# First tiles of two experts drawn from token tiles 0 to 5 and multiplied between the last token tile's routing steps

## The chip, the core and the metric

The kernel runs on one core of one Trainium2 chip. The metric is the device time of one execution in microseconds (us): the median of three runs before the change is 941.35, from 939.15 to 944.55. The engines of the core are TensorE (PE in the profile), VectorE (DVE), ScalarE (ACT), GpSimd (POOL) and SyncE (SP). Each runs its own queue of instructions in order; they wait for one another through semaphores. DMAs are issued from the queues of SP, ACT and POOL.

## What is computed

One decoder layer on 1024 tokens of 1024 features. Three mixers (gated linear attention, a convolution, differential attention) read one projection; their outputs are projected back and added to `x`. Then each token is routed to two of 16 experts: the best group of four by one set of logits, then the two best experts in it.

```python
x = x + mix @ w_out
t = rms_norm(x, ffn_norm_g)
# top-1 group of glog, then top-2 experts inside it, weights top_p
for e in range(16):
    hid = silu(t @ w_gate[e]) * (t @ w_up[e])
    y = y + gates[:, e:e + 1] * (hid @ w_down[e])
x = x + y
```

## The kernel before

**Token tiles.** Everything behind the mixers works on eight tiles of 128 tokens. `out_proj` projects one tile; tiles 0 to 2 are fillers in the attention, tiles 3 to 7 run in a loop at the end of `hybrid_kernel`. While tile i is projected, a table `at` calls the routing of the tiles before at given positions among its matmuls: `out_tr` transposes the normed tokens, `out_logits` multiplies them with the router (`plg`), `route_pick` takes the logits `L`, the experts as one-hot rows `O`, and their sum `M`. `route_rank` counts with a matmul (`pr`) how many earlier tokens chose the same expert; `route_slot` turns the rank into one-hot rows `oh` and writes, with matmuls into `pi` and `pst` (`route_static`), which token sits in which slot. For the last tile all this comes behind its projection, and then `route_tab` and `route_map` build the tables of the tiles.

**Expert tiles.** The experts work on 23 tiles of 128 slots, in an order written as a string: P is an expert with a pair of tiles, S an expert with one. The first tile of each of the first `NSTAT` experts is static (its expert is known when the program is built); the others get their expert at run time. One tile is: a gather of 128 tokens by POOL (`moe_gather`, tile `xg`), transposes (`moe_xt`, `pt` to `xT`), 24 matmuls of 128x512 for gate and up (`moe_gu`, `pgu`), `moe_ht`, 12 matmuls for down (`moe_down`, `py`), the weighting into `y`, and a scatter by POOL that adds `y` to the output. The scatters add to the same array, so each waits until the one before has landed.

**Weights.** An expert has three matrices of 1 MB. Each is loaded as `mraw` and split into a high and a low part in fp32r (`mw`): ACT casts a half of 1024 columns (L129), DVE subtracts it (L130), and POOL does one such subtraction of a down matrix. Static experts are loaded through SP, the others through POOL. Ten `mraw` buffers (two pools of 6 and 4) let the loads run three experts ahead of the tiles; there are four pairs of `mw` buffers.

**What sets the order.** TensorE's instructions stand in the order in which the code is written. For the other engines a scheduler orders them by priority when the program is built; `high_priority(offset=-LATER)` puts work behind what is urgent. Once built, the order on each engine is fixed: a load behind a scatter on POOL is issued after that scatter.

Of the kernel before, what the change touches and what calls it, by code (L numbers as in the profile page):

```python
# [18 lines left out]
S = 1024  # L19
D = 1024  # L20
NT = 8
# [3 lines left out]
NSTAT, NPAIR, NSING = 4, 4, 11  # L25
NALW = 2 * NPAIR + NSING
NDYN = NALW + 8
# [9 lines left out]
EARLY = (True, False)  # L37
SP_LOADS = True
# [5 lines left out]
ORDER = 'PSSPSSPSSPSSSSS'  # L44
# [6 lines left out]
RAW_B = 4  # L51
# [6 lines left out]
EX0 = 'Pvvv'  # L58
# [877 lines left out]
def route_consts(K):  # L936
# [24 lines left out]
    v.memset(K.sacc, 0.0)  # L961
    K.selS = c.tile([128, NSTAT], FT, name="selS")
# [9 lines left out]
    v.tensor_scalar(K.e128, pf[:, 1:2], 16.0, None, op0=OP.mult)  # L972
# [20 lines left out]
def route_pick(K, i):  # L993
# [23 lines left out]
    v.tensor_tensor(T.O, K.iota[:, :16].unsqueeze(1).to_broadcast([128, 2, 16]),  # L1017
# [22 lines left out]

def route_rank(K, i):
# [3 lines left out]
    pr = K.psum.tile([128, 512], FT, name="pr", tag="acc", bufs=2)  # L1045
# [42 lines left out]
def route_static(K, i):  # L1088
    T, v = K.ot[i], K.nc.vector
    ps = K.psum.tile([128, 512], FT, name="pst", tag="acc", bufs=2)  # L1090
# [38 lines left out]
def route_map(K):  # L1129
# [6 lines left out]
    sx = c.tile([128, 128], BF, name="seenx", bufs=1)  # L1136
# [41 lines left out]
    K.slots = tables(K, K.selS, NSTAT, "s", K.sg) + K.slots  # L1178
# [7 lines left out]
def raw_tile(K):  # L1186
    rp = K.ring[K.nraw % len(K.ring)]
    K.nraw += 1
    return rp.tile([128, 2048], FT, name="mraw")


def mw_pair(K):
    return [K.mw.tile([128, 4, 2, 256], FR, name=f"mw{x}") for x in range(2)]
# [50 lines left out]
def moe_gather(K, j):  # L1244
    nc = K.nc
    xg = K.xpage.tile([128, D], FT, name="xg", tag="pg")
    K.last_gather = nc.gpsimd.indirect_dma_start(out=xg, out_offset=None, in_=K.td,
# [17 lines left out]
def moe_gu(K, W, xT, mid):  # L1265
    nc, mp = K.nc, K.mp
    ps = K.psum.tile([128, 512], FT, name="pgu", tag="acc", bufs=2)
# [6 lines left out]
    nc.scalar.activation(sg, ps[:, :256], AF.Silu)  # L1274
# [34 lines left out]
def moe_run(K, tiles, ex, main):  # L1309
# [7 lines left out]
    def gather(a):  # L1317
        if a < n:
            xg[a] = moe_gather(K, tiles[a][1])
# [15 lines left out]
    for a in range(3):  # L1335
        gather(a)
    if main:
        late = route_map(K)
        next(late)
        xT[0] = moe_xt(K, xg[0], 2)  # L1340
    with ExitStack() as st:
        for ins in [K.last_gather] + ([K.last_tab] if main else []):
            st.enter_context(K.tc.issue_after(ins))
        for l in range(3):
            loads(l)
        splits(0)
        loads(3)
        splits(1)
        if not main:
            loads(4)  # L1350
    if not main:
        xT[0] = moe_xt(K, xg[0], 2)
    for a in range(n + 1):
        if a < n:
            def mid(m):
                if main and a == 0 and m == MAP_AT:
                    run(late)
                    loads(4)
                if m == HT_AT and a > 0:
# [11 lines left out]
        if a > 0 and (a != n - 1 or DOWN_AT is None):  # L1371
            down(a - 1)
        if a + 2 in begins:
            loads(begins[a + 2] + 3)
# [35 lines left out]
def hybrid_kernel(ctx, tc, inp, out):  # L1410
# [106 lines left out]
    K.ring = [A] * RAW_A  # L1517
    K.nraw = K.nmw = 0
    g = nc.gpsimd
    ex = [Expert(K, e) for e in range(4)]  # L1520
    loads = [(x, a) for x in ex for a in range(3)]
    for x, a in loads[:RAW_A]:
        x.load(a)
    L = NT - 1
    done = 0
    for i in range(NFILL, NT):
        if i + 1 < NT:
            out_prep(K, i + 1, K.page)
        if i == L - 1:
            sx.close()  # L1530
            B = pool(K, so, "mrawB", RAW_B, side="right")
            K.ring += [B] * RAW_B
            for x, a in loads[RAW_A:RAW_A + RAW_B]:
                x.load(a)
# [3 lines left out]
        if done < i - 1:  # L1538
            at[30] = [lambda k=done: route_rank(K, k)]
            at[44] = [lambda k=done: route_slot(K, k)]  # L1540
            done += 1
        if i == L:
            at[34] = [lambda: out_tr(K, L, K.page2, ((0, 4),))]
            at[42] = [lambda: out_logits(K, L, range(0, 4))]
            at[40] = [lambda: route_rank(K, L - 1)]
            at[58] = [lambda: out_tr(K, L, K.page2, ((4, 6),))]
            at[62] = [lambda: route_slot(K, L - 1)]
            at[66] = [lambda: out_logits(K, L, range(4, 6))]
        run(out_proj(K, i, K.page, K.page, True, at))
    out_tr(K, L, K.page2, ((6, 8),))  # L1550
    out_logits(K, L, range(6, KT))
    route_pick(K, L)
    out_last(K)
    route_rank(K, L)
    route_slot(K, L)
    route_tab(K)
    K.slots = [(K.sg[:, a:a + 1],) for a in range(NSTAT)]
    sl.close()
    with ExitStack() as s1:
        K.mw = pool(K, s1, "mwp", 4)  # L1560
        K.mp = pool(K, s1, "mp")
        K.xpage, K.ypage, K.ny = K.page, K.page2, 0

        with tc.issue_after(K.last_exp):
            nc.scalar.preload_act_table_set("silu_and_others")
        def ex0(hf):
            with tc.high_priority(offset=-LATER):
                ex[0].split_gu([{'P': (g, True), 'p': g, 'v': None}[e] for e in EX0], (hf,))

        def gated(hf):  # L1570
            with tc.issue_after(K.last_exp), tc.issue_after(K.last_pool), tc.issue_after(K.last_route):
                ex[0].split_gu([{'P': (g, True), 'p': g, 'v': None}[e] for e in EX0], (hf,))

        for hf in range(2):
            (ex0 if EARLY[hf] else gated)(hf)
        if SP_LOADS:
            for x, a in loads[RAW_A + RAW_B:]:
                x.load(a)
# [30 lines left out]
```

## Time and profile before

| what | value |
|---|---|
| median of three runs | 941.35 us (939.15 to 944.55) |
| profiled execution, its own time | 940.18 us |
| its span in the profile | 938.6 us |
| mean granted clock of TensorE, share of full | 0.931 |
| busy: PE, DVE, ACT, POOL | 818.2, 649.2, 493.7, 165.0 us |
| moved by the DMA engines | 119.29 MB |

The span is the stretch between the first and the last instruction that the profiler recorded; the execution's own time is 1.6 us longer. The busy times are sums over the whole span; what matters for a change is which engine waits in its stretch. The last projected tile ends near 660 us; the expert stage runs from there to the end.

### The profile page before, as it was taken

The page shows a single profiled execution, that of the slowest core. Times are in us where ns is not written, and L with a number is a line of the kernel's source. Part 1 is how long each engine was busy: PE and PEld are TensorE (multiplying, and loading weights), DVE is VectorE, ACT ScalarE, POOL GpSimd, SP SyncE. Part 2 cuts the span into 40 slices and gives each one's busy share as a digit, 9 for nine tenths or more (in the row PEclk, how much of TensorE's full clock was granted, in tenths as well). Part 3 has the DMA queues.
Part 4 walks back from the last instruction along what each step waited for, and adds up shares of the span by engine and source line. Part 5 has one row for each costly group of instructions (what it writes and reads, how often), then busy time and mean ns, then how long its engine had stood idle before and what let it go on. Part 6 is the DMA issues. An engine that isn't in the chain of part 4 may idle for free. (4 is left out here: it accounts for less than half of the span.)

```text
span 938.6 us, 14319 instructions
## 1 busy us (share of the span) xinstructions
PE 818.2 (87%) x5256; PEld 717.1 (76%) x5256; DVE 649.2 (69%) x1441; ACT 493.7 (53%) x1094; POOL 165.0 (18%) x165
## 2 busy tenths in 40 slices
PE   5999999789768998899878899999399999999870
PEld 4999989688658987788767688888278888888750
DVE  6841556988997666768857666666868677687850
ACT  6743516124246565667757554232558667677730
POOL 5100000000000000000000000000537666664221
PEclk9999989669879999999988999999689999999995
DMA  8210101102002002001202218434479999998942
GB/s 261 76 44 2 46 1 28 37 1 63 6 0 69 1 1 68 1 1 41 68 22 59 81 68 348 168 151 187 170 275 344 335 358 305 363 328 273 318 69 45
DMA packets 46007, 119.29 MB, mean 127 GB/s; under 512 B 6670, under 2 KB 26220, under 8 KB 38636
## 3 DMA queue, kind: packets, MB, share of 16 engines
q0 software_dynamic: 13104, 71.31, 23.0%
q1 hardware_dynamic: 28876, 41.15, 13.2%
q10 hardware_dynamic: 3952, 5.86, 1.7%
q8 instruction: 43, 0.70, 0.3%
q14 instruction: 32, 0.26, 0.1%
HBM read 97.33 MB, written 20.97 MB: 126 GB/s over the span
## 5 line engine op out<-in xcount | busy, mean ns | idle before, releaser
L1272 PE MATMUL pgu<-mw,xT 128*128 128x512 f32 x552 | 140.9, 404 | 0.8 <-ACT xT L129 0.8
L130 DVE TENSOR_TENSOR mw<-mraw,mw 128x1024 fp32r<-128x1024 f32 x99 | 120.9, 1256 | 11.3 <-ACT mw L129 10.4
L1272 PEld LDWEIGHTS pgu<-mw,xT 128*128 128x128 f32 x552 | 102.8, 190 | 24.9 <-issue 1.2
L129 ACT ACTIVATE mw<-mraw 128x1024 fp32r<-128x1024 f32 x113 | 112.9, 1052 | 14.4 <-PE pgu L1272 14.4
L251 PE MATMUL psA<-wh,hnh 128*128 128x384 f32 (+1 forms) x320 | 110.2, 344 | 1.0 <-ACT wh L129 1.0
L251 PE MATMUL psA<-wh,hnl 128*128 128x384 f32 (+1 forms) x320 | 110.6, 346 | 0.2 <-DVE xra L110 0.2
L251 PE MATMUL psA<-wl,hnh 128*128 128x384 f32 (+1 forms) x320 | 109.7, 343 | 0.9 <-DVE wl L130 0.9
L881 PE MATMUL psO<-woh,mx 128*128 128x512 f32 (+1 forms) x272 | 86.8, 396 | 3.5 <-DVE mx L130 2.5
L586 DVE SCALAR_TENSOR_TENSOR mix<-mix,par 128x994 f32<-128x994 f32 (+29 forms) x60 | 75.7, 1262 | 2.1 <-ACT mix L583 1.3
L942 POOL IOTA iota<- 128x128 f32 x1 | 0.2, 238 | 434.9 <-DVE mix L614 434.9
L1300 PE MATMUL py<-mw,hT 128*128 128x512 f32 x276 | 67.3, 392 | 4.5 <-DVE y L1304 2.9
L1300 PEld LDWEIGHTS py<-mw,hT 128*128 128x128 f32 x276 | 51.7, 188 | 16.7 <-ACT hT L129 3.9
L251 PEld LDWEIGHTS psA<-wh,hnh 128*128 128x128 f32 x320 | 63.2, 198 | 1.6 <-ACT wh L129 1.3
L251 PEld LDWEIGHTS psA<-wl,hnh 128*128 128x128 f32 x320 | 63.2, 197 | 1.3 <-DVE wl L130 1.2
L251 PEld LDWEIGHTS psA<-wh,hnl 128*128 128x128 f32 x320 | 63.1, 197 | 0.6 <-DVE hnl L130 0.4
L718 DVE TENSOR_REDUCE nm<-sc 128x1 f32<-128x128 f32 (+7 forms) x64 | 46.8, 751 | 21.7 <-PE sc L714 17.8
L720 ACT ACTIVATE e<-sc,nm 128x128 f32<-128x128 f32 (+7 forms) x64 | 47.3, 740 | 25.6 <-DVE nm L718 21.8
L881 PEld LDWEIGHTS psO<-woh,mx 128*128 128x128 f32 x272 | 49.8, 192 | 12.9 <-DVE mx L130 2.9
L260 PE MATMUL psA<-hnh,wl 128*128 128x256 f32 x192 | 57.1, 297 | 0.0
L260 PE MATMUL psA<-hnl,wh 128*128 128x256 f32 x192 | 57.0, 297 | 0.0
L260 PE MATMUL psA<-hnh,wh 128*128 128x256 f32 x192 | 56.1, 292 | 0.2 <-DVE mix L556 0.2
L881 PE MATMUL psO<-wol,mx 128*128 128x512 f32 (+1 forms) x136 | 53.5, 394 | 0.0
(388 smaller groups left out, 1841.8 us busy)
## 6 DMA issues: line engine op xcount, KB each, us to landing
mraw<-in_expert_w_gate_dram POOLq DMA_DIRECT2D x15, 1024.0 KB, 9.1
mraw<-in_expert_w_up_dram POOLq DMA_DIRECT2D x15, 1024.0 KB, 10.2
mraw<-in_expert_w_down_dram POOLq DMA_DIRECT2D x15, 1024.0 KB, 15.2
wraw<-in_w_in_dram SPq DMA_DIRECT2D x64, 128.0 KB
mix<-in_x_dram SPq DMA_DIRECT2D x8, 512.0 KB
wraw<-in_w_out_dram SPq DMA_DIRECT2D x16, 256.0 KB
h<-in_x_dram SPq DMA_DIRECT2D x8, 512.0 KB
out_dram<-h SPq DMA_DIRECT2D x8, 512.0 KB
```

Source lines behind the costliest of these rows:

```text
L129: K.nc.scalar.activation(hi, src, AF.Copy)
L130: (eng or K.nc.vector).tensor_tensor(lo, src, hi.bitcast(FT), op=OP.subtract)
L251: nc.tensor.matmul(ps[:, :n], a[:, k, cs], b[:, k % 2, :n], start=(k == 0 and t == 0), stop=(k == KT - 1 and t == 2))
L260: nc.tensor.matmul(ps, a[:, k % 2, c0:c0 + 128], b[:, k, :], start=(k == 0 and t == 0), stop=(k == KT - 1 and t == 2))
L586: nc.vector.scalar_tensor_tensor(y[:, sh:], z[:, :S - sh], w(t), y[:, sh:], op0=OP.mult, op1=OP.add)
L718: nc.vector.tensor_reduce(nm, scs[m][:, :n], axis=AX.X, op=OP.max, negate=True)
L720: nc.scalar.activation(e[:, :n], scs[m][:, :n], AF.Exp, bias=nm, accum_out=sums[:, u, m:m + 1])
L881: nc.tensor.matmul(ps, a[:, k, :], b[:, k % 4, c0 % 512:c0 % 512 + c1 - c0], start=(k == 0 and t == 0), stop=(k == KT - 1 and t == 2))
L942: g.iota(t, allow_small_or_imprecise_dtypes=True, **kw)
L1272: nc.tensor.matmul(ps, a[:, k, :], b[:, k % 4].rearrange("p a f -> p (a f)"), start=(n == 0), stop=(n == 23))
L1300: nc.tensor.matmul(py[:, c * 512:(c + 1) * 512], a[:, k, :], b[:, k, c * 512:(c + 1) * 512], start=(k == 0 and t == 0), stop=(k == 1 and t ...
```

## The change

The experts are renumbered by a rotation of ten (`ROT`), so that experts 10 to 15 come first; six are static instead of four, and nine single tiles are dynamic instead of eleven. The sum stays 23 tiles. The first tiles of the first two experts are drawn from token tiles 0 to 5 alone (`ECUT`): `route_static` adds up the slots of these in `eacc` with two further fp32 matmuls for each of the six tiles; `route_cut` raises the two experts' counts to a full tile of 128 behind tile 5; `route_early` makes the slots, and two gathers follow while tile 6 is projected. The ranks of tiles 5 and 6 move to an earlier place. `moe` then starts with the gate and up matmuls of these two tiles, and the routing of the last token tile is called between them (`mid0`, `mid1`). There is one pool of six `mraw` buffers, so that loads run two experts ahead; `mw` has six pairs. The splits of experts 0 and 1 and the loads of experts 2 and 3 stand in `hybrid_kernel`; the shares of POOL in expert 0's gate and up splits are gone.

```diff
-NSTAT, NPAIR, NSING = 4, 4, 11
+NSTAT, NPAIR, NSING = 6, 4, 9
+NEARLY, ECUT, ROT = 2, 6, 10
-ORDER = 'PSSPSSPSSPSSSSS'
+ORDER = 'PSSPSSPSSPSSS'
-RAW_B = 4
...
+def route_cut(K):
+    nc, v = K.nc, K.nc.vector
+    pe = K.psum.tile([128, 512], FT, name="pcut", tag="tr")
+    nc.tensor.matmul(pe[:, :16], K.ones, K.seen[:, ECUT, :], start=True, stop=True)
+    d = K.rt.tile([128, NEARLY], FT, name="cutd", bufs=1)
+    v.tensor_scalar(d, pe[:, :NEARLY], -1.0, 128.0, op0=OP.mult, op1=OP.add)
+    v.scalar_tensor_tensor(K.seen[0:1, ECUT, :NEARLY], d[0:1], 0.0, K.seen[0:1, ECUT, :NEARLY], op0=OP.max, op1=OP.add)
...
 def route_static(K, i):
+    early = i < ECUT
     for s in range(2):
-        K.nc.tensor.matmul(ps[:, :NSTAT], T.oh[0][:, s, :], T.os[:, s, :], start=(s == 0), stop=(s == 1))
+        K.nc.tensor.matmul(ps[:, :NSTAT], T.oh[0][:, s, :], T.os[:, s, :], start=(s == 0), stop=(s == 1 and not early))
+    if early:
+        for s in range(2):
+            K.nc.tensor.matmul(ps[:, NSTAT:NSTAT + NEARLY], T.oh[1][:, s, :], T.os[:, s, :NEARLY].bitcast(FT),
+                               start=False, stop=(s == 1))
...
     if main:
+        L = NT - 1
+        xg.update(enumerate(K.xge))
+        xT[0] = K.xt0
+
+        def mid0(m):
+            if m == 4:
+                out_tr(K, L, K.page2, ((6, 8),))
+                out_logits(K, L, range(6, KT))
+                route_pick(K, L)
+                out_last(K)
+            if m == 12:
+                xT[1] = moe_xt(K, xg[1])
+
+        def mid1(m):
+            if m == 2:
+                route_rank(K, L)
+            if m == 12:
+                hid[0] = moe_ht(K, hid[0])
+            if m == 18:
+                route_slot(K, L)
+                route_tab(K)
+                K.slots = K.eslots + [(K.sg[:, a:a + 1],) for a in range(NEARLY, NSTAT)]
+                for a in range(NEARLY, 5):
+                    gather(a)
+
+        hid[0] = moe_gu(K, ex[0].W, xT[0], mid0, wait=lambda: K.last_exp)
+        splits(2)
+        static(4)
+        hid[1] = moe_gu(K, ex[1].W, xT[1], mid1, True)
         late = route_map(K)
         next(late)
+        down(0)
+        splits(3)
+        static(5)
+        hid[1] = moe_ht(K, hid[1])
+        down(1)
+        xT[2] = moe_xt(K, xg[2], 2)
...
         if a + 2 in begins:
-            loads(begins[a + 2] + 3)
+            loads(begins[a + 2] + 2)
...
         if i == L - 1:
             sx.close()
-            B = pool(K, so, "mrawB", RAW_B, side="right")
-            K.ring += [B] * RAW_B
-            for x, a in loads[RAW_A:RAW_A + RAW_B]:
-                x.load(a)
+            K.mwe = pool(K, so, "mwe", 4, side="right")
+            with tc.high_priority(offset=-LATER):
+                ex[0].split_gu()
+                for a in range(2):
+                    ex[2].load(a)
...
-        if done < i - 1:
+        if done < i - 1 or i == L - 1:
             at[30] = [lambda k=done: route_rank(K, k)]
             at[44] = [lambda k=done: route_slot(K, k)]
...
-        K.mw = pool(K, s1, "mwp", 4)
+        K.mw = pool(K, s1, "mwp", 8)
...
+        with tc.high_priority(offset=-LATER):
+            ex[0].split_d((None, None))
+            ex[2].load(2)
+            ex[1].split_gu()
+            for a in range(2):
+                ex[3].load(a)
+            ex[1].split_d((None, None))
+            ex[3].load(2)
         moe(K, ex)
```

The built programs show two places where instructions moved. The first is DVE's queue behind the last token tile's projection; `h` adds the projection's second half, `L` are its logits, `mw<-mraw,mw` is one subtraction of a split. Before:

```order
L889 TENSOR_TENSOR h<-psO_7453,h 128x256
L130 TENSOR_TENSOR mw_7595<-mraw,mw_7594 128x4x256
L897 TENSOR_TENSOR hsum<-hsum,hs 128x1
L107 TENSOR_SCALAR hrv<-hsum 128x1
L109 SCALAR_TENSOR_TENSOR hra<-hry 128x1
L110 TENSOR_TENSOR hra<-hra,hrv 128x1
L112 SCALAR_TENSOR_TENSOR hr<-hra,hry 128x1
L933 SCALAR_TENSOR_TENSOR L<-plg,hr,rb 128x24
```

After the change, from `hrv` on (two more subtractions and `h` stand just ahead):

```order
L104 TENSOR_SCALAR hrv<-hsum 128x1
L127 TENSOR_TENSOR mw_7587<-mraw,mw_7586 128x4x256 x2
L127 TENSOR_TENSOR mw_7593<-mraw,mw_7592 128x4x256 x2
L127 TENSOR_TENSOR mw_7697<-mraw,mw_7696 128x4x256 x2
L106 SCALAR_TENSOR_TENSOR hra<-hry 128x1
L127 TENSOR_TENSOR mw_7603<-mraw,mw_7602 128x1024 x2
L107 TENSOR_TENSOR hra<-hra,hrv 128x1
L127 TENSOR_TENSOR xT<-pt,xT 128x1024
L127 TENSOR_TENSOR mw_7703<-mraw,mw_7702 128x4x256
L109 SCALAR_TENSOR_TENSOR hr<-hra,hry 128x1
L127 TENSOR_TENSOR mw_7703<-mraw,mw_7702 128x4x256
L930 SCALAR_TENSOR_TENSOR L<-plg,hr,rb 128x24
```

One subtraction stood between `h` and `L`; now there are twelve, and a half of `xT`.

The second place is POOL's queue in the expert stage, one cycle of four tiles; `out_dram<-y` is a scatter, `xg` a gather, `mraw` a load. Before, from the loads behind scatter S5 to scatter S7:

```order
L1212 ISA
L1212 DMA mraw<-in_expert_w_gate_dram 128x2048
L1212 ISA
L1212 DMA mraw<-in_expert_w_up_dram 128x2048
L1212 ISA
L1212 DMA mraw<-in_expert_w_down_dram 128x2048
L130 TENSOR_TENSOR mw_8361<-mraw,mw_8360 128x1024
L1305 DMA out_dram<-y,os 1152x1024
L1247 DMA xg<-td,og 128x1024 x3
L1305 DMA out_dram<-y,os 1152x1024
```

After the change, from the gather ahead of scatter S4 to the loads behind S5:

```order
L1283 DMA xg<-td,og 128x1024
L1349 DMA out_dram<-y,ss 1152x1024
L127 TENSOR_TENSOR mw_8363<-mraw,mw_8362 128x1024
L1349 DMA out_dram<-y,ss 1152x1024
L1246 TENSOR_LOAD erow
L1246 ISA x2
L1248 ISA
L1248 DMA mraw<-in_expert_w_gate_dram 128x2048
L1248 ISA
L1248 DMA mraw<-in_expert_w_up_dram 128x2048
L1248 ISA
L1248 DMA mraw<-in_expert_w_down_dram 128x2048
```

Before, three gathers stood between the two scatters that have no loads between them; now nothing but a subtraction stands there, and the cycle's gathers stand with loads: in the next group, behind S6, three loads and three gathers.

## Rows read from the trace of the kernel before

The times are those of the profiled execution. Lines as L1305 are lines of the kernel before.

**Rows 1.** The chain that ended last: start us, us, what.

```profile
915.49 1.55 DMA out_dram<-y,os
```

**Rows 2.** All instructions on out_dram: from a scatter's issue to its landing.

```profile
DMA to landing us min/median/max: 6.3/9.0/11.9
```

**Rows 3.** Timeline of POOL: the scatters into out_dram.

```profile
738.03 2.53 POOL L1305 DMA_INDIRECT out_dram<-y,ss  x1 [1.99 <-DMA out_dram<-y,ss]
...
746.72 1.62 POOL L1305 DMA_INDIRECT out_dram<-y,os  x1 [0.30 <-DVE xT L130]
...
759.45 1.66 POOL L1305 DMA_INDIRECT out_dram<-y,os  x1 [3.08 <-DVE mw L130]
...
769.26 1.67 POOL L1305 DMA_INDIRECT out_dram<-y,os  x1 [3.33 <-DMA out_dram<-y,os]
...
779.12 2.01 POOL L1305 DMA_INDIRECT out_dram<-y,os  x1 [3.93 <-DVE sg L1275]
...
787.74 1.63 POOL L1305 DMA_INDIRECT out_dram<-y,os  x1 [0.30 <-DVE mw L130]
...
799.18 2.10 POOL L1305 DMA_INDIRECT out_dram<-y,os  x1 [4.84 <-DVE mw L130]
...
870.39 1.65 POOL L1305 DMA_INDIRECT out_dram<-y,os  x1 [3.45 <-DVE hT L130]
...
899.37 3.65 POOL L1305 DMA_INDIRECT out_dram<-y,os  x1 [5.12 <-DVE y L1304]
...
922.18 1.55 POOL L1305 DMA_INDIRECT out_dram<-y,os  x1 [5.14 <-issue]
```

**Rows 4.** Timeline of PE in the expert stage: two neighbouring tiles, and a wait.

```profile
768.70 2.98 PE L1272 MATMUL pgu<-mw,xT 128*128 128x512 f32 x12
...
778.19 2.98 PE L1272 MATMUL pgu<-mw,xT 128*128 128x512 f32 x12
...
883.02 3.00 PE L1300 MATMUL py<-mw,hT 128*128 128x512 f32 x12 [2.86 <-DVE y L1304]
```

**Rows 5.** Windows: sum, then busy (instructions) PE, PEld, DVE, ACT, POOL, clock, DMA, GB/s.

```profile
670.00:680.00 10.00, 2.60 (x15) 2.39 (x15) 9.56 (x16) 4.85 (x6) 7.66 (x5) 0.50 0.74 275
...
700.00:720.00 20.00, 20.00 (x98) 16.67 (x97) 17.64 (x20) 17.12 (x23) 12.88 (x11) 1.00 1.01 370
```

**Rows 6.** Timeline of PE: start us, us, line, operation, out<-in, [idle before].

```profile
646.36 1.86 PE L930 MATMUL plg<-wr,hT 128*128 128x24 f32 x16
...
659.82 0.28 PE L881 MATMUL psO<-woh,mx 128*128 128x256 f32 x1
...
682.53 3.75 PE L1272 MATMUL pgu<-mw,xT 128*128 128x512 f32 x8 [0.78 <-ACT xT L129]
...
688.61 1.04 PE L1258 MATMUL pt<-ident,xg 128*128 128x128 f32 x8
689.41 5.86 PE L1272 MATMUL pgu<-mw,xT 128*128 128x512 f32 x24
...
699.50 2.90 PE L1300 MATMUL py<-mw,hT 128*128 128x512 f32 x12
702.24 2.98 PE L1272 MATMUL pgu<-mw,xT 128*128 128x512 f32 x12
```

**Rows 7.** All instructions on mraw: ns min/median/max of the two halves of a split.

```profile
L130 DVE TENSOR_TENSOR mw<-mraw,mw x99: 1210/1217/4057, 660.5 to 900.4; 128x1024 fp32r<-128x1024 f32 x99
```

**Rows 8.** Timeline of DVE around the last token tile.

```profile
660.13 0.42 DVE L889 TENSOR_TENSOR h<-psO,h 128x256 f32<-128x256 f32 x1 [2.34 <-PE psO L881]
...
665.08 0.24 DVE L933 SCALAR_TENSOR_TENSOR L<-plg,hr,rb 128x24 f32<-128x24 f32 x1
...
666.95 0.17 DVE L1020 TENSOR_TENSOR M<-O 128x16 bf16<-128x16 f32 x1
```

**Rows 9.** Timelines of DVE and POOL: two subtractions side by side.

```profile
676.39 4.06 DVE L130 TENSOR_TENSOR mw<-mraw,mw 128x1024 fp32r<-128x1024 f32 x1
677.01 2.35 POOL L130 TENSOR_TENSOR mw<-mraw,mw 128x1024 fp32r<-128x1024 f32 x1
```

More of the change, by code (lines that the diff above doesn't have):

```diff
@@ L1044, in route_rank @@
     T = K.ot[i]
[L1045 removed]
+    pr = K.psum.tile([128, 512], FT, name="pr", **route_tag(i))
     nc.tensor.matmul(pr[:, :16], K.tri, T.M, start=True, stop=(i == 0))
@@ L1186, in raw_tile @@
 def raw_tile(K):
-    rp = K.ring[K.nraw % len(K.ring)]
-    K.nraw += 1
-    return rp.tile([128, 2048], FT, name="mraw")
+    return K.mraw.tile([128, 2048], FT, name="mraw")
 def mw_pair(K):
-    return [K.mw.tile([128, 4, 2, 256], FR, name=f"mw{x}") for x in range(2)]
+    p = K.mwe if K.nmw % 6 < 2 else K.mw
+    K.nmw += 1
+    return [p.tile([128, 4, 2, 256], FR, name=f"mw{x}", tag="mw") for x in range(2)]
 class Expert:
@@ L1262, in moe_xt, with moe_gu @@
     return xT
-def moe_gu(K, W, xT, mid):
+def moe_gu(K, W, xT, mid, wide=False, wait=None):
     nc, mp = K.nc, K.mp
-    ps = K.psum.tile([128, 512], FT, name="pgu", tag="acc", bufs=2)
+    if wide:
+        ps = K.psum.tile([128, 1024], FT, name="pguw", tag="sc")[:, :512]
+    else:
+        ps = K.psum.tile([128, 512], FT, name="pgu", tag="acc", bufs=2)
     order = [(k, t) for hf in range(2) for t in range(2) for k in range(hf * 4, hf * 4 + 4)] + [(k, 2) for k in range(KT)]
@@ L1273, in moe_gu @@
     sg = mp.tile([128, 256], FT, name="sg", bufs=2)
-    nc.scalar.activation(sg, ps[:, :256], AF.Silu)
+    if wait is not None:
+        with K.tc.issue_after(wait()):
+            nc.scalar.preload_act_table_set("silu_and_others")
+            nc.scalar.activation(sg, ps[:, :256], AF.Silu)
+    else:
+        nc.scalar.activation(sg, ps[:, :256], AF.Silu)
     nc.vector.tensor_tensor(sg, sg, ps[:, 256:], op=OP.mult)
@@ L1317, in gather @@
     def gather(a):
-        if a < n:
+        if a < n and a not in xg:
             xg[a] = moe_gather(K, tiles[a][1])
@@ L1333, in down, with static @@
         moe_down(K, ex[tiles[a][0]].W, hid[a], tiles[a][1], main and a >= n - END_PAGE)
-    for a in range(3):
-        gather(a)
+    def static(l):
+        with K.tc.high_priority(offset=-LATER):
+            for a in range(len(ex[l].raws), 3):
+                ex[l].load(a)
     if main:
+        L = NT - 1
[24 more added lines that the diff above has]
+        hid[1] = moe_gu(K, ex[1].W, xT[1], mid1, True)
@@ L1338, in moe_run @@
         late = route_map(K)
         next(late)
-        xT[0] = moe_xt(K, xg[0], 2)
[L1341 to L1353, printed above, removed]
+        down(0)
+        splits(3)
@@ L1354, in moe_run @@
+        static(5)
+        hid[1] = moe_ht(K, hid[1])
+        down(1)
+        xT[2] = moe_xt(K, xg[2], 2)
+    else:
+        for a in range(3):
+            gather(a)
+        loads(0)
+        loads(1)
+        splits(0)
+        loads(2)
+        splits(1)
+        loads(3)
+        xT[0] = moe_xt(K, xg[0], 2)
+    for a in range(2 if main else 0, n + 1):
         if a < n:
             def mid(m):
-                if main and a == 0 and m == MAP_AT:
+                if main and a == 2 and m == MAP_AT:
@@ L1357, in mid @@
                     run(late)
-                    loads(4)
-                if m == HT_AT and a > 0:
+                if m == HT_AT and a - 1 in hid and not (main and a == 2):
                     hid[a - 1] = moe_ht(K, hid[a - 1])
@@ L1516, in hybrid_kernel, with early, early_xt @@
         route_pick(K, i)
-    K.ring = [A] * RAW_A
-    K.nraw = K.nmw = 0
+    K.mraw = A
+    K.nmw = 0
     g = nc.gpsimd
-    ex = [Expert(K, e) for e in range(4)]
-    loads = [(x, a) for x in ex for a in range(3)]
-    for x, a in loads[:RAW_A]:
-        x.load(a)
+    ex = [Expert(K, (e + ROT) % NE) for e in range(NSTAT)]
+    for x in ex[:RAW_A // 3]:
+        for a in range(3):
+            x.load(a)
     L = NT - 1
     done = 0
+    K.xpage, K.ypage, K.ny = K.page, K.page2, 0
+    def early():
+        K.eslots = K.slots = route_early(K)
+        K.xge = [moe_gather(K, a, ECUT * 128) for a in range(NEARLY)]
+    def early_xt():
+        K.xt0 = moe_xt(K, K.xge[0])
     for i in range(NFILL, NT):
```

74 lines of the change are left out of this document (37 added, 37 removed).

## The prediction, made before the changed kernel ran

> **What bounds the kernel now.** I went from the end backwards. The chain of waits ends in the scatters of the expert stage [rows 1]: POOL adds the tokens of one expert tile to the output, and each scatter is issued only when the one before has landed, 6.3 to 11.9 us after its issue [rows 2]. I number the 23 scatters S0 to S22; the rows show S3 to S9, S16, S19 and S22. Between S4 and S16, 12 scatters take 870.39 - 746.72 = 123.67 us, 41.2 us for four [rows 3]. TensorE needs 778.19 - 768.70 = 9.49 us for a tile, 38.0 for four [rows 4]. So the scatters fall behind TensorE by 3.2 us in every four tiles, until TensorE waits for them at 883 (2.86 us behind DVE's `y`, whose page the scatters had not yet left) [rows 4]. The last scatter is issued at 922.18, whatever TensorE does after its last tile. The windows show the other place where time is lost: from 670 to 680 TensorE works 2.60 of 10 us, at half clock; from 700 on it has no gap, while the DMA engines are full (share 1.01, 370 GB/s) [rows 5]. The reader is to see two resources there: a gap of TensorE before the expert stage, which the change aims at, and a queue of transfers behind it, which sets the end.
>
> **Part 1, up to the last output matmul.** It ends at 659.82 + 0.28 = 660.1 [rows 6]. Added ahead of it are: (a) two fp32 matmuls of two columns in each of tiles 0 to 5, 12 in all. They are not in the trace. Sixteen records of `plg`, fp32 with 24 columns, take 1.70 us up to the next start, and one instruction is two records [rows 6], so 0.21 each, 2.5 together; from below 0 (they hide between waits), from above 2.5; I take 2.5 since the matmuls around them leave no gap. (b) The eight transposes of the first expert tile, 689.41 - 688.61 = 0.8 [rows 6], which leave the gap. (c) The rank of tile 5 moves into tile 6, whose position 30 TensorE reaches while DVE has four halves of expert 0 ahead of tile 5's logits, 4 x 1.217 = 4.9 us [rows 7]. How much of this TensorE waits is between 0 and 4.9; ahead of that position stand 30 matmuls, at 5.86 / 24 = 0.24 each 7.3 us, that cover most of it, so I take 1.5. Sum: 660.1 + 4.8 = 664.9. The additions on DVE and the two early gathers lie beside matmuls; without that cover they would cost some 3 us.
>
> **Part 2, the gap.** Before, `L` of the last token tile starts 5.0 us after 660.1, `M` at 666.95 [rows 8], and the third expert tile starts at 702.24 [rows 6], 42.1 after 660.1. In the change the DVE queue holds 12 subtractions of splits between the last `h` and that `L` (ten in the rows shown of the order, two ahead of them), where there was one, and the lower half of `xT`. Twelve more at 1.217 are 14.6 [rows 7]; I take off 3 for the waits on ACT that DVE has between `h` and `L` today and that the splits fill, so `L` comes at 664.9 + 5.0 + 11.5 = 681.4 and `M` 1.9 later, 683.3. TensorE has the first tile's 24 matmuls for this time (5.6 at full clock, 11.3 at the 0.47 of eight in 3.75 [rows 6]); then it stands until `M`, as before. Then come the rest of the second tile (22 matmuls, 5.2 to 10.3, taken as 7), twice 2.90 for `py` [rows 6], and the transposes, copies and waits between: at least three groups of transposes at 0.8, 2.4, at most two waits of 4.06 more [rows 9], 10.5; I take 8.4, near the upper bound, since DVE is busy 9.56 of 10 us there already before [rows 5]. Sum 704.5, between 698 and 710. So the gap is filled with two tiles, but its end is not earlier: +2.3 us. TensorE then has one `py` of 2.90 less ahead than before at this point. **The entry to the expert loop is about even.**
>
> **A rule against the row, on the gap.** In the trace a DVE subtraction that stood beside one of POOL took 4.06 us instead of 1.22 [rows 7, 9]. The Trainium skill, "SBUF — State Buffer", section "SBUF: two separate sides", says that DVE, with two inputs in SBUF, and GpSimd share a pair of ports as an exclusive lock, so that whichever starts first holds off the other for its whole length. The change keeps one POOL subtraction ahead of the gathers of tiles 2 to 4; by that rule this could delay them by up to 2.8 us, and the sum below would be 954 instead of 951. I leave it out, since the rule gives no order of the two.
>
> **Part 3, the expert stage, which sets the end.** I read what stands between two scatters on POOL, and what it made of the next interval (all loads, gathers and scatters that POOL issues share one queue, so a scatter lands behind the loads ahead of it). After an interval with three loads: 9.81 and 9.86 (S5 to S6, S6 to S7). After three loads and one gather: 12.73 and 11.44 (S4 to S5, S8 to S9), mean 12.1. After three gathers alone: 8.62 (S7 to S8). After nothing: (922.18 - 899.37) / 3 = 7.6 [rows 3]. The four make the old cycle: 12.7 + 9.8 + 9.9 + 8.6 = 41.0. It agrees with the bytes: a load is 1.05 MB, at 370 GB/s 2.8 us [rows 5], three and a scatter of 0.52 MB 9.9.
>
> The order of the change on POOL shows other groups: loads run two experts ahead instead of three, out of six raw pages instead of ten. From S3 on a cycle is now three loads and a gather, **nothing**, three loads, then **three loads and three gathers**. The gathers that used the interval without loads now stand in one with loads. Two gathers more cost between 2 x 0.4 (three gathers alone cost 8.6 - 7.6) and 2 x 2.3 (12.1 - 9.8); by bytes 2 x 1.4 = 2.8, which I take. Cycle: 12.1 + 7.6 + 9.8 + 14.9 = 44.4, from below TensorE's 38.0, from above 46.2. Three cycles from S4 to S16: 133.2 against 123.67, **+9.5**.
>
> The end: behind S16 there are now loads of the last expert after S17 instead of after S16. 9.8 + 7.6 + 9.8 + 3 x 7.6 = 50.0 against 922.18 - 870.39 = 51.8: **-1.8**. The start: S3 now has loads, three gathers and a POOL subtraction ahead of it; S4 between -2 and +7 us, I take **+3.3** from one interval of 12.1 where 8.7 was (S3 to S4, 746.72 - 738.03 [rows 3]). The loads of two more experts go over SP and come before; the bytes are the same. The Trainium skill, "DMA: Bandwidth & Descriptors", section "Issuing engines are not separate DMA queues", says that transfers of all engines end up on the same 16 DMA engines; no run here shows the two queues side by side in this stage. By it the move to SP gains nothing, which the share of 1.01 [rows 5] supports.
>
> **Sum.** +3.3 + 9.5 - 1.8 = +11.0. The profiled execution took 940.18 (1.2 below the median of 941.35): 951.2, **951**. TensorE will wait more often for a free `y` page, but its waits are inside this chain.
>
> **Rivals.** (A) The cycle keeps its length, because the loads, issued earlier in some intervals, fill the empty one: 940.2 + 3.3 - 1.8 = 941.7. For it: the bytes are the same, and the DMA engines were already full. Against: POOL issues in order, and nothing stands between those two scatters. Chance 0.20. (B) The gap really closes, and the result is faster: if the 12 subtractions don't hold `L` (because their casts and loads are early and DVE runs through them while TensorE is still in tile 7), 11.5 us go from the gap; the scatters start that much earlier, and with the old cycle the end is 940.2 - 8 = 932. The point that decides is `L` of the last tile: under 8 us behind the last output matmul it is this. Against: `h`, which stands ahead of them on DVE, itself waits for that matmul [rows 8]. Chance 0.10. (C) Six raw pages starve the splits: an expert's loads are issued two tiles, 19.0 us, ahead of use, and the longest group in the queue is 14.9 by part 3; a wait of 2 us in each of the nine single tiles is +18 for TensorE, of which the scatters hide half: 960. Against: the wait at 883 is for `y`, none in the rows is for a load. Chance 0.15. (D) The change doesn't do what it says: a token count beyond the 23 tiles would start the loop for the rest, another expert with some 28 us (12.1 + 9.5 + 7): 968. Nothing in the trace tells it. Chance 0.02. The forecast has 0.53.
>
> **How the numbers follow.** About 0.5% (4.7 us) is what a measurement of this kernel can tell from no change: faster is under 936.6, slower over 946.1. Faster: B, 0.10. Same: A and the low edge of the forecast (a cycle of 42.5 gives 945), 0.22. Slower: 0.68. The range takes A's upper half, the forecast with gathers at both bounds (945 to 957) and C: 940 to 961; outside are B, D and part of A.
>
> **What would show it.** `L` of the last token tile 14 to 18 us behind the last output matmul, not 5; the third expert tile at 701 to 709; a stretch of half clock as long as before; four scatters in 43 to 46 us from S4 to S16, with one interval near 7.6 and one near 15 in each; the loads of the last expert behind S17; the last scatter near 933. If four scatters take 41 us, part 3 is wrong and A holds; if the third tile starts before 696, part 2 is wrong and B holds; if splits wait for loads, C.

## The result and the profile after the change

The changed kernel takes **952.19 us** in the median (949.18 to 954.66) beside 940.25 for the kernel before in the same comparison: a ratio of **1.0138 [1.0103, 1.0174]** (the brackets are a 95% interval), slower by 12 us in the medians and some 13 by the ratio. The prediction was 951, between 940 and 961. The profiled execution took 954.66 (span 952.8), the longest of four and 14.5 more than the profiled one before. Shown are, of both, the places that the prediction named:

| place | before | after | predicted for after |
|---|---|---|---|
| end of the last output matmul | 660.1 | 665.1 | 664.9 |
| `L`, `M` of the last token tile | 665.1, 667.0 | 681.2, 683.1 | 681.4, 683.3 |
| third expert tile starts | 702.2 | 706.4 | 704.5 |
| scatter S4 | 746.7 | 752.4 | 750.0 |
| S4 to S16, twelve scatters | 123.7 | 133.4 | 133.2 |
| S16 to S22 | 51.8 | 51.0 | 50.0 |
| S22 to the end of the execution | 18.0 | 17.8 | not named |

The differences, +5.0 up to the last output matmul, -0.8 from there to the third tile, +1.5 to S4, +9.7, -0.8 and -0.2, make the 14.4 that the profiled executions lie apart.

**The entry.** Timeline of PE in the kernel after the change (start, length, line, operation, idle time before it with its releaser):

```profile
640.67 0.18 PE L1076 MATMUL pr<-M,tri 128*128 128x16 bf16 x1 [1.82 <-DVE M L1025]
...
664.84 0.28 PE L878 MATMUL psO<-woh,mx 128*128 128x256 f32 x1
664.95 1.10 PE L1311 MATMUL pgu<-mw,xT 128*128 128x512 f32 x4
...
683.35 0.19 PE L1076 MATMUL pr<-M,tri 128*128 128x16 bf16 x1 [7.09 <-DVE M L1025]
...
698.55 1.19 PE L1344 MATMUL py<-mw,hT 128*128 128x512 f32 x4 [2.25 <-ACT hT L126]
700.34 3.66 PE L1344 MATMUL py<-mw,hT 128*128 128x512 f32 x8 [0.60 <-DVE hT L127]
...
706.42 2.12 PE L1311 MATMUL pgu<-mw,xT 128*128 128x512 f32 x8 [1.54 <-ACT xT L126]
```

The first expert's matmuls follow the projection at once; later TensorE stands for 7.09 us until `M`. The last row is the start of the third tile. Timeline of DVE over the same time, and the POOL rows that belong to its last one:

```profile
668.56 6.89 DVE L127 TENSOR_TENSOR mw<-mraw,mw 128x1024 fp32r<-128x1024 f32 x6
...
681.24 0.24 DVE L930 SCALAR_TENSOR_TENSOR L<-plg,hr,rb 128x24 f32<-128x24 f32 x1
...
683.12 0.17 DVE L1025 TENSOR_TENSOR M<-O 128x16 bf16<-128x16 f32 x1
...
689.02 3.23 DVE L127 TENSOR_TENSOR mw<-mraw,mw 128x1024 fp32r<-128x1024 f32 x1
...
688.78 2.38 POOL L127 TENSOR_TENSOR mw<-mraw,mw 128x1024 fp32r<-128x1024 f32 x1 [21.49 <-PE pguw L1311]
692.59 0.96 POOL L1283 DMA_INDIRECT xg<-td,sg  x1 [1.43 <-DVE seenx L1173]
```

`L` stands behind the subtractions, as the order said. The 3.23 us of a subtraction beside POOL's answer to the 4.06 of [rows 9]. Two windows of the stretch (columns as in [rows 5]):

```profile
670.00:680.00 10.00, 3.73 (x16) 2.41 (x15) 10.00 (x11) 7.36 (x9) 0.00 (x0) 0.82 0.90 329
680.00:690.00 10.00, 6.65 (x31) 5.58 (x31) 7.83 (x37) 6.07 (x11) 1.22 (x1) 0.67 0.89 341
```

DVE has no gap from 670 to 680, TensorE works 3.73 us of these ten. The granted clock is 0.82 and 0.67 in the mean of these windows, a mixture of its two levels, 1.2 and 2.4 GHz, where [rows 5] had 0.50 in the first. In windows of 2.5 us it is under full from 662.5 to 687.5 before, and from 675 to 687.5 and 700 to 705 after, behind the waits of TensorE. So the stretch at the lower level is shorter than before, while the prediction had it as long.

**The scatter cycle.** Timeline of POOL from S4 to S9, then S16 and S22, where [rows 3] has those of before:

```profile
752.42 1.64 POOL L1349 DMA_INDIRECT out_dram<-y,ss  x1 [1.06 <-DMA out_dram<-y,ss]
...
764.18 2.05 POOL L1349 DMA_INDIRECT out_dram<-y,ss  x1 [5.86 <-DVE mw L127]
765.73 1.12 POOL L1248 DMA_DIRECT2D mraw<-in_expert_w_gate_dram  x1
766.32 1.10 POOL L1248 DMA_DIRECT2D mraw<-in_expert_w_up_dram  x1
766.88 1.06 POOL L1248 DMA_DIRECT2D mraw<-in_expert_w_down_dram  x1
771.45 1.66 POOL L1349 DMA_INDIRECT out_dram<-y,os  x1 [3.51 <-DVE xT L127]
...
777.82 1.01 POOL L1283 DMA_INDIRECT xg<-td,og  x1 [0.30 <-issue]
779.14 0.97 POOL L1283 DMA_INDIRECT xg<-td,og  x1 [0.30 <-issue]
780.42 1.93 POOL L1283 DMA_INDIRECT xg<-td,og  x1 [0.31 <-PE pt L1294]
782.65 1.62 POOL L1349 DMA_INDIRECT out_dram<-y,os  x1 [0.30 <-DVE hT L127]
...
797.06 2.47 POOL L1349 DMA_INDIRECT out_dram<-y,os  x1 [2.15 <-DMA out_dram<-y,os]
...
808.08 1.58 POOL L1349 DMA_INDIRECT out_dram<-y,os  x1 [6.11 <-DVE sg L1319]
...
885.81 2.36 POOL L1349 DMA_INDIRECT out_dram<-y,os  x1 [7.73 <-DVE mw L127]
...
936.84 1.55 POOL L1349 DMA_INDIRECT out_dram<-y,os  x1 [5.16 <-DMA out_dram<-y,os]
```

The three loads stand before S6, three loads (left out) and three gathers before S7, and no transfer stands between S4 and S5. The releasers named are often engines that had long been done: ten of the twelve scatters from S5 to S16 are issued 4.6 us or more behind their `y`, and the wait is for the landing. S7 and S14 are issued 0.5 and 0.3 us behind their `y`, so there the tile may have set the issue. Grouped by what was issued ahead of the interval's first scatter, the twelve intervals from S4 to S16 are:

| ahead | after, three each | predicted |
|---|---|---|
| three loads, one gather | 11.76, 11.02, 12.17 | 12.1 |
| nothing | 7.27, 7.11, 8.69 | 7.6 |
| three loads | 11.20, 11.36, 9.91 | 9.8 |
| three loads, three gathers | 14.41, 13.50, 14.99 | 14.9 |

**What the new order wastes.** The same window of both kernels; the first row is of before, the second of after (columns as in [rows 5]):

```profile
760.00:820.00 60.00, 60.00 (x296) 50.09 (x295) 42.80 (x49) 39.93 (x52) 40.70 (x30) 1.00 1.00 349
```

```profile
760.00:820.00 60.00, 57.68 (x274) 47.98 (x273) 40.48 (x43) 34.32 (x45) 33.53 (x28) 0.97 0.86 288
```

Before, the DMA engines are full all the time. After, they have 0.86 and 288 GB/s. Where nothing stands between two scatters they run dry: from 762 to 766, on both sides of the issue of S5, their share is 0.02, and from 806 to 810, around S9, again. The groups that follow are so much the larger. Part of what an empty interval saves is paid in the next, which has three loads ahead: the two together take 18.5, 18.5 and 18.6 us, where the prediction had 7.6 + 9.8 = 17.4.

### The profile page after: what moved, and what is told of

The parts are those of the page before. It is cut to its first block, busy times and chain, and to the rows that moved or that the text cites. A ratio compares the mean times of both kernels' runs of the same rounds, so it can differ in the third digit from the quotient of the medians.

```text
span 952.8 us, 14375 instructions
## 1 busy us (share of the span) xinstructions
PE 825.8 (87%) x5281; PEld 723.6 (76%) x5281; DVE 661.5 (69%) x1460; ACT 494.5 (52%) x1095; POOL 149.8 (16%) x156
## 3 DMA queue, kind: packets, MB, share of 16 engines
q0 software_dynamic: 12240, 65.02, 21.2%
## 5 line engine op out<-in xcount | busy, mean ns | idle before, releaser
L127 DVE TENSOR_TENSOR mw<-mraw,mw 128x1024 fp32r<-128x1024 f32 x102 | 135.3, 1365 | 31.8 <-ACT mw L126 24.4
L1311 PE MATMUL pgu<-mw,xT 128*128 128x512 f32 x528 | 134.8, 404 | 1.5 <-ACT xT L126 1.5
L1311 PEld LDWEIGHTS pgu<-mw,xT 128*128 128x128 f32 x528 | 99.3, 192 | 23.5 <-ACT xT L126 1.7
L1344 PE MATMUL py<-mw,hT 128*128 128x512 f32 x276 | 72.6, 414 | 10.1 <-ACT hT L126 4.6
L1344 PEld LDWEIGHTS py<-mw,hT 128*128 128x128 f32 x276 | 54.4, 200 | 24.2 <-ACT hT L126 5.4
```

What stands on the lines that cost most here:

```text
L127: (eng or K.nc.vector).tensor_tensor(lo, src, hi.bitcast(FT), op=OP.subtract)
L1311: nc.tensor.matmul(ps, a[:, k, :], b[:, k % 4].rearrange("p a f -> p (a f)"), start=(n == 0), stop=(n == 23))
L1344: nc.tensor.matmul(py[:, c * 512:(c + 1) * 512], a[:, k, :], b[:, k, c * 512:(c + 1) * 512], start=(k == 0 and t == 0), stop=(k == 1 and t ...
```

## The experiments

Ratios are to the kernel before, measured beside it, whose median lay between 936.89 and 942.6 in these comparisons. S0 to S22 are the scatters, a cycle is four of them.

**1. The same kernel with other pages for y.** One number moves the gathers back into the interval without loads.

```diff
-YP = [0, 0, 0, 1]
+YP = [0, 1, 0, 0]
```

> The changed kernel with one table shifted by two places: of four y tiles the second, not the fourth, takes its page from the pool of the gathers. On POOL this puts two gathers into the interval between two scatters that was empty, and takes the three gathers out of the crowded one; loads, raw pages and all matmuls stay. Theory G (grouping on POOL sets the scatter chain): a cycle of four scatters from S4 on falls from 44.5 to 41 or 42 us, three cycles give 5 to 9 us, about 945 us against 952 for the change. Rival S (six raw pages starve the splits): the loads are issued as before, the time stays within 2 us of 952.

Measured: 947.75, ratio 1.0073 [1.0036, 1.0110], 4.4 us less than the change has by the medians and 6 by the ratios. Timeline of POOL, the scatters S4 to S8:

```profile
755.27 1.68 POOL L1349 DMA_INDIRECT out_dram<-y,ss  x1 [4.93 <-DVE y L1348]
...
764.75 1.62 POOL L1349 DMA_INDIRECT out_dram<-y,ss  x1 [0.15 <-issue]
...
772.74 1.64 POOL L1349 DMA_INDIRECT out_dram<-y,os  x1 [0.30 <-issue]
...
785.95 1.66 POOL L1349 DMA_INDIRECT out_dram<-y,os  x1 [6.87 <-DVE xT L127]
...
796.80 2.37 POOL L1349 DMA_INDIRECT out_dram<-y,os  x1 [2.03 <-DVE y L1348]
```

A cycle takes 41.5, 40.7 and 40.3 us: an interval behind two or three gathers alone 8.0 to 8.5, behind three loads 9.5 to 10.9, behind three loads with gathers 12.4 to 13.2. The cycles together gave back 133.4 - 122.5 = 10.9 us; 2.9 of it went again since S4 came later, most of that already ahead of the last output matmul (667.5). Same number of transfers, same bytes, six raw pages in both: what stands with what is the cause of the longer cycle.

**2. The counterpart.** The same line in the kernel before puts its gathers with loads.

> The kernel before with the same table shifted by two places. On POOL one interval of a cycle is now empty and another holds three loads and two gathers, as in the changed kernel; it keeps ten raw pages, loads three experts ahead and its old gap. Theory G: the cycle rises from 41.2 to 44 us, the time by 7 to 10 us to about 949. Rival S: raw pages and lookahead are as they were, the time stays within 2 us of 940.

Measured: 953.05, ratio 1.0121 [1.0071, 1.0170]. Two of three cycles take 44.7 and 44.9 us, the third 40.9. The time came out 4 us above theory G's 949. So one number makes the old kernel as slow as the change, without any of its other edits.

**3 and 4. Scatters that need not wait for one another.** Each expert tile scatters into an array of its own, so that the experts' outputs are left out of the result; otherwise all work stays.

```diff
+    dst = K.dram.tile([S + 128, D], FT, name=f"scr{K.ny}") if K.ny <= 23 else K.out
-    K.last_gather = nc.gpsimd.indirect_dma_start(out=K.out, ...
+    K.last_gather = nc.gpsimd.indirect_dma_start(out=dst, ...
```

> The changed kernel with every scatter adding into an array of its own, so that no scatter waits for the one before; the expert outputs are left out of the result. Theory G: TensorE sets the end. Its last tile starts near 706 + 20 x 9.5 = 896, the last scatter is issued near 912 instead of 937, and the time is about 929. Rival S: waits for loads stay in TensorE's way, 938 or more.

> The kernel before with every scatter adding into an array of its own; the expert outputs are left out of the result. Theory G: the third tile starts at 702 as before and TensorE runs without the wait at 883, the last scatter near 908 instead of 922, about 926 us; so the two kernels without the chain lie some 3 us apart, the difference at the entry, instead of 12. Rival S: the distance of 12 stays.

Measured: the changed kernel 933.82, ratio 0.9917 [0.9887, 0.9947]; the kernel before 927.39, ratio 0.9839 [0.978, 0.9899]. The chain of scatters costs the changed kernel 1.0138 - 0.9917 = 2.2%, 21 us, and the one before 1.6%, 15. By these ratios 6 of the 13 us are the chain's, as in experiment 1, but their intervals leave that uncertain by about as much. Some 6 to 7 remain without the chain, twice theory G's 3: the third tile is 2.1 us later (705.2 and 703.1), and behind it TensorE is 208.8 us, not 204.6, from done. In that stretch its waits add up to 5.8 us, most of them for `sg` and `y`, and to 2.2 in the kernel before; what makes them longer is not tested. What lies outside the cycles the prediction had put at +1.5 (S4 +3.3, tail -1.8).

**5 and 6. The loads on another queue.** The loads of experts chosen at run time are issued by SP; gathers and scatters stay with POOL.

```diff
-    engines=(mybir.EngineType.Pool,),
+    engines=(mybir.EngineType.SP,),
-            self.load(a, self.K.nc.gpsimd)
+            self.load(a, self.K.nc.sync)
```

> The changed kernel with the loads of the experts chosen at run time issued from SP's queue instead of POOL's; scatters and gathers stay on POOL, the bytes are the same. Theory Q (a scatter lands behind the loads that stand ahead of it in the same queue): without them an interval costs what the empty ones cost in the changed kernel, 7.1 to 8.7 us (up to 9 with three gathers), four scatters some 31 to 33, less than TensorE's 38, so the chain no longer sets the end; the time is that of the kernel whose scatters do not wait for one another, about 934, and splits wait for loads as little as there (3 us instead of 16.7). Rival B (bytes: all transfers share the same DMA engines, so it does not matter from which queue they come): four scatters in 43 to 46 as before, 952 within 3.

> The kernel before with the same move of the loads to SP's queue. Theory Q: about 928, as where its scatters do not wait for one another (927.4); four scatters in 38, set by TensorE. Rival B: 941 within 3, four scatters in 40 to 43. In both, the distance to the changed kernel on SP tells what the change costs without the chain: 6 to 7 us by the runs without the chain.

Measured: 951.29, ratio 1.0117 [1.0069, 1.0166], and for the kernel before 945.38, ratio 1.0041 [1.0007, 1.0075]. Nothing is gained that can be told, and before loses a little. The landing of the scatters, first of the changed kernel, then of the same with its loads on SP:

```profile
DMA to landing us min/median/max: 6.0/8.3/11.4
```

```profile
DMA to landing us min/median/max: 6.1/9.0/13.8
```

Two windows of the latter:

```profile
760.00:820.00 60.00, 57.38 (x271) 47.14 (x270) 45.63 (x47) 38.55 (x50) 27.77 (x16) 0.97 1.00 345
...
880.00:930.00 50.00, 41.86 (x189) 33.55 (x187) 27.68 (x32) 22.48 (x32) 11.38 (x7) 0.97 0.56 120
```

From 760 to 820 the DMA engines are now full (1.00, 345 GB/s), no split waits for a load, and still four scatters take 46.7, 45.1 and 41.0 us. What the loads take early, the scatters wait for. The six last intervals, with hardly a load left, take 44.0 instead of 51.0, but S4 comes 5.1 us later, and the median is the same. In the kernel before the move makes the cycles longer, 43.5, 46.8 and 41.7 us instead of 41.0, 39.5 and 43.2, and S4 14.6 us later; its last six intervals take 42.8 instead of 51.8. So theory Q falls, and rival B holds for the changed kernel, while the kernel before is 1.4 us over B's range. The Trainium skill, "DMA: Bandwidth & Descriptors", section "Issuing engines are not separate DMA queues", says that transfers of all engines share the same 16 DMA engines, and these runs agree. So my words that a scatter lands behind the loads of its own queue were too narrow: loads from another queue hold it up as well. Within POOL's queue the order does count: three loads issued 1.6 to 2.7 us behind S5 left that interval at 7.27.

**7. Every y in its own pool.** `YP = [0, 0, 0, 0]` spreads the gathers evenly.

> The changed kernel with every y in its own pool of pages (none in the gathers' pool), which spreads the gathers of a cycle: three loads and one gather, one gather alone, three loads, three loads and two gathers. It measures what a gather beside loads costs. If 2.3 us each (from three loads 9.8 and with one gather 12.1), a cycle is 12.1 + 8.0 + 9.8 + 14.4 = 44.3, no change, 952 within 2. By the intervals of the changed kernel and of the one with its pages shifted (11.9, 7.9, 10.3, 13.2) it is 43.3, 948 to 949. If a gather costs only its bytes, 1.4 each, 11.2 + 8.0 + 9.8 + 12.6 = 41.6, about 944.

The cycles take 42.1, 42.5 and 41.5 us, nearest to the price by bytes (41.6). Their single intervals don't bear it out: three loads alone took 12.40 and 12.14, three loads with two gathers 11.72 and 11.74. So the sum fits, and the price of a gather stays open. Behind an empty interval or a lone gather, three loads cost more than the 9.8 that was read from intervals behind a full one; why is not shown. The time does not show the shorter cycles: 952.3, ratio 1.0103 [1.0057, 1.0149]. In its profile the last output matmul ended at 670.4, 5.3 later than in the changed kernel, though the instructions up to there are the same, and already some 5 later at 605. The time is inconclusive.

**8. No subtraction of POOL ahead of the gathers.**

```diff
-        splits(2)
+        ex[2].splits(True)
```

> The changed kernel with the last half of expert 2's down split on DVE instead of POOL: nothing is left on POOL ahead of the gathers of tiles 2 to 4. Theory L (the two subtractions side by side hold each other off: in the changed kernel DVE's took 3.23 us beside POOL's 2.38, ahead of the tables): the tables and the third gather come 2.0 us earlier, the third tile at 704.4 instead of 706.4, and the scatters behind it with it: 950. Rival N (DVE is full there, and the subtraction that it takes over costs 1.2 before the third tile): third tile at 705 to 707, 952 within 1.

Timelines of DVE, POOL and PE of this kernel:

```profile
688.77 2.35 DVE L127 TENSOR_TENSOR mw<-mraw,mw 128x1024 fp32r<-128x1024 f32 x2
...
691.47 0.96 POOL L1283 DMA_INDIRECT xg<-td,sg  x1 [24.42 <-DVE seenx L1173]
...
704.03 2.14 PE L1311 MATMUL pgu<-mw,xT 128*128 128x512 f32 x8 [1.82 <-ACT xT L126]
```

DVE does two subtractions in 2.35 us, where one beside POOL's had taken 3.23; the gathers start 1.1 us earlier and the third tile 2.4, with the last output matmul at the same place (664.9). That is theory L's number, but only half of it is L's. From `M` to the third tile it is 21.2 us here and 23.3 in the changed kernel. In experiments 1, 3 and 5, which keep POOL's subtraction there, it is 22.3; the difference to the changed kernel is a `py` that ran at the lower clock in the profiled execution (from 700.0 to 702.5 granted 0.56, in experiment 3 1.00; 3.66 us at 700.34 above). The same eight matmuls in experiment 3:

```profile
700.36 2.12 PE L1344 MATMUL py<-mw,hT 128*128 128x512 f32 x8 [0.60 <-DVE hT L127]
```

So the subtraction is worth 1.1 us at the third tile, and the clock 1.0. The execution did not get faster: 954.97, ratio 1.0147 [1.0107, 1.0188]. So the local cost is shown, and that it reaches the end is not.

**9. The logits ahead of the splits.** The splits of experts 0 and 1, with their loads, are called behind `out_last` in `mid0`, and the tables earlier.

```diff
             if m == 4:
...
+                with K.tc.issue_after(K.last_exp), K.tc.high_priority(offset=-LATER):
+                    ex[1].split_gu()
+                    ex[0].split_d((None, None))
...
+            if m == 22:
+                route_rank(K, L)
-            if m == 18:
+            if m == 8:
```

> The changed kernel with the splits of experts 0 and 1 put behind the logits of the last token tile in DVE's order (the loads of expert 2's down and of expert 3 move with them), and the tables called earlier. Theory O (the twelve subtractions ahead of L set the end of the gap by their order): L near 671 instead of 681.2, M near 673, the third tile some 8 us earlier, 698, and the end with it: 944. Rival T (DVE's work sets it, in whatever order: the same splits must be done before the first two tiles are, and the tables after them): L near 671, but the third tile at 704 to 708 as before, TensorE waiting for splits instead of M; 952 within 3.

Timelines of DVE and PE, and the POOL row beside the second DVE row:

```profile
672.60 0.24 DVE L930 SCALAR_TENSOR_TENSOR L<-plg,hr,rb 128x24 f32<-128x24 f32 x1
...
699.26 3.06 DVE L1189 SCALAR_TENSOR_TENSOR mt<-ma,mapv 128x1 f32<-128x1 f32 x1
...
699.93 2.36 POOL L127 TENSOR_TENSOR mw<-mraw,mw 128x1024 fp32r<-128x1024 f32 x1
...
707.33 3.78 PE L1344 MATMUL py<-mw,hT 128*128 128x512 f32 x8 [4.83 <-DVE hT L127]
...
713.50 2.12 PE L1311 MATMUL pgu<-mw,xT 128*128 128x512 f32 x8 [0.69 <-ACT xT L126]
```

`L` comes 2.7 us behind the last output matmul (669.9 here) instead of 16.1. The third tile comes 43.6 behind it, not 41.3: the wait for `M` is gone, and TensorE waits for `xT`, splits and `hT` instead. Some 2.5 of the 43.6 are the clock, granted 0.51 from 703.0 to 713.5 (eight matmuls of `py` 3.78 us instead of 2.1, eight transposes 1.91 instead of 1.04). Rival T's mechanism holds: DVE works 36.0 us between the last output matmul and the third tile, 35.5 of the 41.3 in the changed kernel, and this order only moved the wait. The time, 957.88, ratio 1.021 [1.0178, 1.0243], is worse than T expected. In the profiled execution, 6.9 us longer than the changed kernel's, 4.8 lie ahead of the last output matmul and 2.3 in the gap; experiment 10, with the same edit, ends that matmul at 665.8, so the 4.8 are not the edit's. The gate loads of later experts, moved with the splits, now make ACT wait 20.3 us where it was 15.0. Why all the runs are slower is open.

**10. Shifted pages, no POOL subtraction and the logits first, together.**

> The same with the y pages shifted as in the changed kernel with its pages shifted, and with expert 2's last down split on DVE instead of POOL. If the parts add up: the shift brought 4.5, the split 0 to 2, the order of the logits nothing (T) or 8 (O): by T 946, by O 938, which would be faster than the kernel before.

Measured: 945.54, ratio 1.009 [1.0061, 1.0118]; cycles of 39.3, 40.0 and 41.3, and the third tile 40.5 behind the last output matmul. It is the number that T gives, but no better by the ratio than the shift alone. No version here that computes the whole result beats the kernel before.

**11. Without the early slots.** The two further matmuls in each of tiles 0 to 5 and the sum in `eacc` are left out, so the tokens of the first two expert tiles are missing from the result. The matmuls have two columns (`pst` 128x2 in the trace), not the six that the expectation names.

```diff
-    if early:
-        for s in range(2):
-            K.nc.tensor.matmul(ps[:, NSTAT:NSTAT + NEARLY], ...
```

> The changed kernel without the twelve fp32 matmuls of six columns and the additions that draw the first two tiles' slots: both tiles then hold empty slots only, whose rows are gathered, multiplied and scattered all the same, so the tokens of two tiles are left out and nothing else. Theory E (the work added ahead of the last output matmul delays everything behind it): by the rows of the changed kernel the matmuls hold TensorE for some 0.45 us in each of six tiles, 2.7 together; the last output matmul ends at 662.4 instead of 665.1, the third tile starts at 703.7 instead of 706.4, S4 at 749.7, and the time is 949.5. Rival H (they are hidden, because the output tiles wait for other work anyway): 665, 706, 952 within 1.

Timeline of PE of the changed kernel (`pi` follows the static matmuls of each tile):

```profile
605.03 1.14 PE L1113 MATMUL pi<-oh,oj 128*128 128x128 f32 x8
...
620.58 1.14 PE L1113 MATMUL pi<-oh,oj 128*128 128x128 f32 x8
...
641.04 0.62 PE L878 MATMUL psO<-woh,mx 128*128 128x512 f32 x2
```

and without the early slots:

```profile
604.02 1.14 PE L1113 MATMUL pi<-oh,oj 128*128 128x128 f32 x8
...
619.12 1.14 PE L1113 MATMUL pi<-oh,oj 128*128 128x128 f32 x8
...
639.15 0.17 PE L1076 MATMUL pr<-M,tri 128*128 128x16 bf16 x1 [2.21 <-DVE M L1025]
...
639.77 1.05 PE L878 MATMUL psO<-woh,mx 128*128 128x512 f32 x2
```

A tile takes 15.10 instead of 15.55 us, so the two matmuls do cost 0.45. TensorE reaches the rank in tile 6 1.5 us earlier (639.15 and 640.67), although it waits 0.4 longer for it. Yet the last output matmul ends at 664.7, only 0.4 earlier: behind that wait the granted clock was 0.66 from 638 to 643 in this execution and 1.00 in the changed kernel's, and the two matmuls shown last took 1.05 us instead of 0.62. That took back 1.1. So H's place for the last output matmul came from the clock, not from H's reason. The third tile (704.7) lies between the two. The time is 951.59, ratio 1.0108 [1.0074, 1.0143], and does not tell E's 949.5 from H's 952.

## Why the prediction held, step by step

- **Part 1** gave 664.9, and it was 665.1. The stall in tile 6 is 1.82 where 1.5 was taken, and term (a) is some 0.45 a tile by experiment 11, 2.7 for 2.5. That the sum fits to 0.2 is luck: in the profiled executions of the changed kernel and of experiments 1, 3, 5, 7 and 8, whose TensorE instructions are the same up to there, the last output matmul ends between 664.9 and 670.4.
- **Part 2** had `L` at 681.4 and `M` at 683.3, both within 0.2. The third tile came at 706.4, not 704.5, and 23.3 us behind `M` instead of 21.2. Of these 2.1 us 1.1 are the subtraction held off by POOL (3.23 instead of 1.22), which the prediction had named and left out; without it experiment 8 has just 21.2. The other 1.0 is the lower clock of that execution. The Trainium skill, "SBUF — State Buffer", section "SBUF: two separate sides", has DVE and GpSimd exclude one another there; the rows agree, in that the DVE operation ends 1.1 us, about its own length, behind POOL's (692.25 and 691.16; in [rows 9] 680.45 and 679.36). The choice to leave it out was a mistake, though the end did not move with it. Experiment 9 shows that an early `L` does not close the gap: the prediction's point for rival B (`L` under 8 us behind) would not have been enough, since with `L` at 2.7 the gap was as long.
- **Part 3** gave 133.2 for S4 to S16, and it was 133.4. Three of its four intervals were within 0.7 of the rows; the one behind three loads alone took 10.8 in the mean instead of 9.8, and the one behind three loads and three gathers 14.3 instead of 14.9. These errors cancel, so the 0.2 is in part luck; the mechanism is not: experiments 1 and 2 show the grouping at work from both sides. What the text got too narrow is the resource: experiments 5 and 6 put the loads on another queue, and the time stayed.
- **The start and the end** were mis-sized: S4 came 5.7 later, not 3.3 (S2 2.4 with the third tile, the two intervals behind it 2.0 and 1.3), and the tail took 0.8 less, not 1.8. The chainless runs tell the same: some 6 to 7 us of the loss remain without the chain. So the parts of the profiled execution make 14.4, not 11.0. That 951 is so near the median of 952.19 is helped by this execution being the longest of the four.
- **Rival A** (the cycle keeps its length) falls with cycles of 44.6, 43.0 and 45.8. **Rival B** falls with `L` 16.1 us behind. **Rival D** falls with 23 scatters. **Rival C** is there in part: ACT's waits in the changed kernel, from 700 on (total, times, longest),

```profile
ACT mw L126 <- DMA mraw<-in_expert_w_gate_dram: 15.0, 6, 4.9
```

and none before. No wait of TensorE there names a split, but what stands behind a waiting cast on ACT, `hT` among it, waits too. Without the chain of scatters the gate loads' share shrinks to 0.7 us, so it follows from loads issued late behind scatters; and with the loads on SP it is gone with the time the same, so these waits alone did not set the end.

## What to carry to other kernels

When a queue of dependent transfers sets the end, list what stands between two of them and price each group from intervals that the trace already shows; a group that is empty saves less than a crowded one costs, and the DMA engines run dry around it. When work is moved into a gap of one engine, add up what the engines that feed it must still do in that gap: here DVE had 35.5 us of work in 41.3, and neither early logits nor late ones made the gap short. A number that only picks a buffer (here one entry of a list of four) can cost as much as a rewrite: 11.6 us in the old kernel, where the whole change costs 12. And a term read off one profiled execution to a fraction of a microsecond wants a second execution beside it: the granted clock alone moved single stretches by 1.0 to 2.5 us here.

## What was not expected of the hardware

An interval with nothing ahead of its scatter takes 7.1 to 8.7 us, and the last three, with nothing else to move, 7.5, 7.8 and 6.7, where the scatter's 0.52 MB at the 349 GB/s of the full window would be 1.5: most of it is not bytes. Moving the loads to another queue did not shorten four scatters. And beside a POOL subtraction of 2.36 us, a DVE operation on 128x1 values took 3.06 us instead of the 0.21 that it takes in experiment 8's kernel: there it was not the size of the DVE operation that counted, but that one was under way on POOL (both end at 702.3). And the granted clock differs between executions of the same instructions: from 700.0 to 702.5 it was 0.56 in the changed kernel and 1.00 in experiment 3.
